# Moving attention's output product ahead of the values' block, and the loads of the input forms to GpSimd's queue

## The chip, the core and the metric

The kernel runs on one core of a Trainium2 chip. The core has TensorE (PE in the profile), VectorE (DVE), ScalarE (ACT), GpSimd (POOL) and SyncE (SP, which here only issues DMAs). Each engine works through its own instructions in a fixed order; they meet through semaphores. The metric is device time in microseconds (us), as the median of several runs. Before the change it is 1493.75 us, from three runs between 1492.93 and 1498.71.

## What is computed

A two-layer decoder over 512 tokens of width 1024, in float32. Each layer projects the normalized input, runs a sliding-window attention and a retention side by side, mixes both through gates, and ends in an MLP:

```python
h = rmsnorm(x, g_mix)
z = h @ w_in
aq, ak, av, rq, rk, rv, rg, ga, gb = jnp.split(z, SPLIT_POINTS, axis=-1)
ya = sliding_window_sink_attention(rope(aq), rope(ak), av, sinks) @ w_a
r = chunkwise_retention(rotate(rq), rotate(rk) * RET_QK_DIM ** -0.5, rv)
r = rms_per_head(r) * silu(rg)
mixed = sigmoid(ga) * ya + sigmoid(gb) * (r @ w_b)
x = x + mixed @ w_out
x = x + jnp.square(jax.nn.relu(rmsnorm(x, g_mlp) @ w_up)) @ w_down
```

A final RMSNorm follows the second layer. `w_in` has 5888 columns, `w_a` is 512 x 1024, and the values `rv` have 1024 columns.

## The kernel before

**Split products.** Every float32 matrix is split into a rounded part (hi) and the remainder (lo), and a product is the sum of three: hi by hi, lo by hi, hi by lo. These are lines 387, 388 and 389 of `products`. ACT rounds (line 335 for weights, 407 and 410 for activations), DVE subtracts (336, 408, 411).

**Weights.** They arrive in units of 128 x 1024 (512 KB) in a fixed order, given by `unit_order`. SP issues a load for each unit four units ahead (`load_until`, line 195, `load_values` line 309); the split runs three units ahead (`split_until`). There are five buffers for raw units and four each for hi and lo.

**Products by blocks.** The values' product and most of the MLP run as a 2 x 2 block product with seven partial products in place of eight. The operands of some of these are sums and differences of quarters of the input and of the weights. The input's quarters for the values' product are made by `Turned`: `load` brings two pairs of input chunks (tile `xg`, 512 KB each, from the input in layer 0 and from a copy in DRAM, `spill`, in layer 1), and `build` scales them on ACT (line 881), forms the combinations on DVE (884 to 887) and splits them (407, 408). There are two loads for `build(0)` and two for `build(2)`. The tiles `xg` share six buffers ("big") with other tiles of a layer: the attention's `whole`, the rg tiles `z`, the decay table `dm`. The weights' sums are made in DRAM by accumulating DMAs on GpSimd's queue (lines 223 and 226); `pace` issues one step of them after every second evacuation, behind a small copy (`mark`, line 247) that waits for that evacuation.

**The order within a layer.** First q, k and v of attention, then gate and retention chunks, between which a generator puts the steps of attention. After the generator is drained come `qk(1)` (retention keys and queries), the filling units rg 4 and 5, then `values` (the seven partial products, each over two units u and two banks m, tile `rv`), then attention's output product with `w_a` (8 products of 12 matmuls, evacuated into the gates on line 1131), and then `qk(2)` and `qk(3)` with the retention of heads 0 and 1 (`score`, `ret` and `r` rows) beside them. A list scheduler places the instructions on each engine by its own estimate of time, within the dependencies and within explicit `issue_after` marks. So the order on each engine isn't the order of the source, but it is fixed when the program is built.

**PSUM.** Eight banks: five in `ps_mm`, three in `ps_aux`. In a block product ACT copies the partial sum `a` into the bank `b` (line 954 for the values, 1405 in the MLP), and later matmuls add to it without opening a new group. A matmul that opens a group first (915 for the values; 1403 in the MLP, for the blocks listed in `CLEANED`) leaves that bank in a state in which they add. In the last layer, `turn_x` transposes x in front of the MLP into two banks, four transposes to a bank (line 1236).

Of the kernel before, what the change touches and what calls it, by code (L numbers as in the profile page):

```python
# [17 lines left out]
P = 128  # L18
# [32 lines left out]
DELAY = 2  # L51
AHEAD = 4
SPLIT = 3
CLEANED = ({1: (0,)}, {0: (0, 1), 1: (0,)})


def unit_order(layer):

    order = [("w_in", i) for i in range(4 + 2 + 8 + 2 + 4 + 2 + 2)]
    order += [("rv", part, u) for part in range(7) for u in range(2)]  # L60
    order += [("w_a", i) for i in range(4)]
    order += [("w_in", i) for i in range(24, 34)]
    order += [("w_b", i) for i in range(4)]
    order += [("w_in", i) for i in range(34, 38)]
    order += [("w_b", i) for i in range(4, 8)]
    order += [("w_out", i) for i in range(8)]
    for e in range(N_BLOCK):
        if e == 0:
            order += [("w_up", u) for u in range(4)]
        else:  # L70
            order += [("pair", 2 * e - 2 + i, part) for i in range(2) for part in range(4)]
        if layer == DEPTH - 1 and e == N_BLOCK - 1:
            order += [("w_end", k) for k in range(4)]
        else:
            order += [("block", e, part) for part in range(7)]
    return order
# [39 lines left out]
def decoder(ctx, tc, xT, x_first, w_in, w_rv, w_a, w_b, w_out, w_up, w_pair, w_down, w_end, tables, decay, band, g_last, out):  # L116
    nc = tc.nc
# [30 lines left out]
    x = little_x[:, P:].rearrange("p (k t) -> p k t", t=T)  # L148
# [13 lines left out]
    order = [(layer, *u) for layer in range(DEPTH) for u in unit_order(layer)]  # L162
# [209 lines left out]
    ident = const.tile([P, P], F32, name="ident")  # L372
# [31 lines left out]
    def split(hi, lo, src, scale=None):  # L404

        if scale is None:
            up = nc.scalar.activation(hi, src, AF.Copy)
            down = nc.vector.tensor_tensor(lo, src, f32(hi), ALU.subtract)
        else:
            up = nc.scalar.activation(hi, src, AF.Copy, scale=scale)  # L410
            down = nc.vector.scalar_tensor_tensor(lo, src, scale, f32(hi), ALU.mult, ALU.subtract)
        return up.ins, down.ins
# [198 lines left out]
    def layer_body(layer):  # L611
# [110 lines left out]
        a_h, a_l = a_t[0][0], a_t[1][0]  # L722

        def attention():
# [18 lines left out]
            def weighted(n):  # L743
                at = slice(n * P, (n + 1) * P)
                both = big("whole")
                rest, whole = both[:, 0, :], both[:, 1, :]
                for g in range(N_KV):
                    own, other = slice(64 * g, 64 * g + 64), slice(64 - 64 * g, 128 - 64 * g)
                    po = bank(ps_aux, "pv")
                    kbs = (1,) if n == 0 else (0, 1)  # L750
                    for kb in kbs:
                        b = n - 1 + kb
                        cols = slice(b * P, (b + 1) * P)
                        p = 2 * g + kb
                        nc.tensor.matmul(po, v_both[g][:, cols], p_h[:, p, :], start=kb == kbs[0], stop=False)
                        nc.tensor.matmul(po, v_high[g][:, cols], p_l[:, p, :], start=False, stop=kb == 1)
                    nc.scalar.activation(rest[own, :], po[other, :], AF.Copy)
                    nc.vector.tensor_tensor(whole[own, :], po[own, :], rest[own, :], ALU.add)
                split(a_h[:, :, at], a_l[:, :, at], whole.rearrange("p (c q) -> p c q", q=P))

            for n in range(NB):
                w = P if n == 0 else 2 * P
# [49 lines left out]
                slots.give(*t[1])  # L812
            slots.give(*k_s, *v_s)

        last_exp = []
        background.append(attention())


# [41 lines left out]
        class Turned:  # L860
# [6 lines left out]
            def load(self, ks):  # L867
                self.b = [big("xg") for _ in range(2)]
                for part, b in enumerate(self.b):
                    k = ks + 4 * part  # L870
                    nc.sync.dma_start(b, source[:, k : k + 2, :])

            def halves(self, ks, which):
                t = self.groups[which][ks // 2][0]
# [36 lines left out]
        def values(turned):  # L911

            a, c = ([bank(ps_mm, "rv") for _ in range(2)] for _ in range(2))
            b = [bank(pool, "rv") for pool in (ps_mm, ps_aux)]
            nc.tensor.matmul(b[1], ones, xh[:, 0, :], start=True, stop=True)
            plus, minus = rms_mix.columns, small.tile([P, NB], F32, tag="ncol", name="ncol", bufs=1)
            nc.vector.tensor_scalar(minus, plus, -1.0, None, ALU.mult)

            def multiply(ps, moving, start=True):
                for u in range(2):  # L920
                    hi, lo = unit("rv", layer)
                    for m in range(2):
                        at = slice(m * P, (m + 1) * P)
                        pairs = []
                        for k in range(2):
                            xh_, xl_ = moving[2 * u + k]
                            cols = slice(k * T, (k + 1) * T)
                            pairs.append(((xh_[:, at], xl_[:, at]), (hi[:, cols], lo[:, cols])))
                        products(ps[m], pairs, start and u == 0, u == 1, not start)

            def scale(j, m, sign):
                return (plus if sign > 0 else minus)[:, 2 * j + m : 2 * j + m + 1]

            def keep(j, ps, sign):
                got = []
                for m in range(2):
                    t = temp("kept")
                    nc.scalar.activation(t, ps[m], AF.Copy, scale=scale(j, m, sign))
                    got.append(t)
                return got  # L940

            def put(i, j, ps, sign, kept=None):
                for m in range(2):
                    hi, lo = slots.one(), slots.one()
                    if kept:
                        nc.vector.scalar_tensor_tensor(kept[m], ps[m], scale(j, m, sign), kept[m], ALU.mult, ALU.add)
                        split(view(hi), view(lo), kept[m])
                    else:
                        split(view(hi), view(lo), ps[m], scale(j, m, sign))
                    rv[i, 2 * j + m] = (hi, lo)  # L950

            multiply(a, quarter(0, 0))
            for m in range(2):
                nc.scalar.activation(b[m], a[m], AF.Copy)
            multiply(c, turned[1])
            five = keep(1, c, -1)
            multiply(b, turned[2], False)
            turned.free(0)
            two = keep(1, b, 1)
            multiply(a, quarter(1, 0), False)  # L960
            put(0, 0, a, 1)
            multiply(c, quarter(1, 1), False)
            put(0, 1, c, 1, two)
            multiply(b, turned[3], False)
            put(1, 1, b, -1, five)
            multiply(b, turned[4], False)
            turned.free(1)
            put(1, 0, b, -1)
# [95 lines left out]
        def load_decay(pair):  # L1064
            decays[pair] = big("dm")
            nc.sync.dma_start(decays[pair], decay[:, 2 * pair : 2 * pair + 2, :])

        def retention(pair):
            two = [Head(2 * pair), Head(2 * pair + 1)]
            for head in two:  # L1070
                for js in ((0, 1), (2, 3)):
                    head.scores(js)
                    yield
            two[0].outputs(0)
            yield
            two[0].outputs(1)
            yield
            two[1].outputs(0)
            yield
            yield  # L1080
            two[0].norm()
            yield
            two[1].outputs(1)
            yield
            yield
            yield
            two[1].norm()
            if pair == 0:
                load_decay(1)
            yield  # L1090
            yield
            while 4 * pair + 3 not in rg:
                yield
            for head in two:
                head.finish()
                yield
# [11 lines left out]
        turned = Turned()  # L1108
        turned.load(0)
        qk(1)  # L1110
        turned.build(0)
        turned.load(2)
        for i in (4, 5):
            chunk("w_in", layer, xs, put_rg(i))
        turned.build(2)
        load_decay(0)
        values(turned)


        aT = [(a_h[:, c, :], a_l[:, c, :]) for c in range(4)]  # L1120
# [12 lines left out]
        for t in a_t:  # L1133
            slots.give(*t[1])

        background.append(retention(0))
        qk(2, 2.0)
        qk(3, 2.0)
# [94 lines left out]

        def turn_x(ps, b, i):
            for k in range(4):
                nc.tensor.transpose(ps[:, k * P : (k + 1) * P], x[:, 4 * i + k, b * P : (b + 1) * P], ident)
            t = temp("y")
            nc.scalar.activation(t, ps, AF.Copy)
            nc.gpsimd.dma_start(y[:, b, i * T : (i + 1) * T], t)
# [542 lines left out]
```

## Time and profile before

| What | Before |
|---|---|
| median of three runs | 1493.75 us |
| the profiled execution, its own time | 1498.12 us |
| its span, first to last instruction | 1496.4 us |
| mean granted TensorE clock | 0.992 |
| DVE busy | 1125.0 us, 75% |
| ACT busy | 943.1 us, 63% |
| POOL busy | 217.4 us, 15% |

In the views quoted below, a row of the timeline gives its start, its duration, the engine, the line of the kernel, the operation, the tile written and the tile read, the shape and the count. A bracket holds the time that the engine sat idle before it and what ended that. In a row of stages, "from:to" is followed by the length of the stage, then busy time and count for PE, PE's weight loads, DVE, ACT and POOL, then the granted clock (1.00 is full), the share of the DMA engines that was busy, and GB/s. A row of waits gives the total in us, how often, and the longest. A row of the chain of work that ended last gives start, duration and what it was. A row for a DMA queue gives packets, MB and the share of 16 engines; a row for DMA issues gives the count, the size and the median time to landing. "q1 hardware_dynamic" carries what SP issues, "q0 software_dynamic" what POOL issues.

### The profile page before, as it was taken

How to read it: one execution, taken by the hardware profiler on the slowest of the kernel's cores; microseconds unless marked ns; L12 is line 12 of the kernel's file. 1: busy time of each engine (PE TensorE's matmuls, PEld its weight loads, DVE VectorE, ACT ScalarE, POOL GpSimd, SP SyncE). 2: the span in 40 equal slices, each digit the busy share in tenths (PEclk: the TensorE clock that was granted, in tenths of full speed). 3: DMA queues.
4: the chain of work that ended last, by engine and by line, in shares of the span. 5: the costliest groups of instructions: out<-in, count | busy, mean ns of one | idle time of the engine just before them, and what ended most of it. 6: DMA issues, size and time to landing. Idle time of an engine off the chain costs nothing.

```text
span 1496.4 us, 21384 instructions
## 1 busy us (share of the span) xinstructions
PE 1464.2 (98%) x7754; PEld 1260.4 (84%) x7754; DVE 1125.0 (75%) x1697; ACT 943.1 (63%) x1549; POOL 217.4 (15%) x294
## 2 busy tenths in 40 slices
PE   9999799999999999999999997999999999999998
PEld 7888588888888999999878885888888889999997
DVE  6878685875577888888778688668756768888885
ACT  7657554553467777777756576455434767777775
POOL 0101101202101111112201011112020021111120
PEclk9999899999999999999999999999999999999999
DMA  7673759568945776666947648677595287776664
GB/s 257 199 202 117 206 169 253 163 187 248 268 119 185 195 193 174 181 179 188 301 168 232 168 134 217 190 206 206 151 284 173 82 214 186 195 196 171 181 192 149
DMA packets 95867, 287.32 MB, mean 192 GB/s; under 512 B 11152, under 2 KB 11280, under 8 KB 90896
## 3 DMA queue, kind: packets, MB, share of 16 engines
q1 hardware_dynamic: 62544, 175.56, 33.6%
q0 software_dynamic: 32496, 109.07, 32.9%
q8 instruction: 61, 1.00, 0.3%
q10 hardware_dynamic: 720, 1.31, 0.2%
q14 instruction: 46, 0.38, 0.1%
HBM read 246.05 MB, written 107.48 MB: 236 GB/s over the span
## 4 chain that ended last, share of the span: by engine, by line
PE 92%; DMA 3%; ACT 2%; DVE 1%; issue 1%; ACTq 0%
PE mm L387 24%; PE mm L388 24%; PE mm L389 24%; PE b L387 3%; PE b L388 3%; PE b L389 3%; DMA xg<-xT_in 2%; PE rv L387 1%; PE rv L388 1%; PE rv L389 1%; PE mm L402 1%; PE score L770 1%; PE pT L735 1%; PE r L388 1%; DMA xg<-spill 1%; PE r L389 1%
## 5 line engine op out<-in xcount | busy, mean ns | idle before, releaser
L335 ACT ACTIVATE hi<-raw 128x1024 fp32r<-128x1024 f32 (+1 forms) x375 | 382.0, 1020 | 308.2 <-PE mm L388 178.4
L336 DVE TENSOR_TENSOR lo<-raw,hi 128x1024 fp32r<-128x1024 f32 (+1 forms) x376 | 438.8, 1174 | 151.4 <-ACT hi L335 150.0
L387 PE MATMUL mm<-xh,hi 128*128 128x512 f32 (+1 forms) x976 | 344.4, 355 | 1.8 <-DVE z L979 1.0
L388 PE MATMUL mm<-xl,hi 128*128 128x512 f32 (+1 forms) x976 | 343.7, 354 | 0.0
L389 PE MATMUL mm<-xh,lo 128*128 128x512 f32 (+1 forms) x976 | 341.9, 355 | 0.0
L388 PE MATMUL mm<-r,hi 128*128 128x256 f32 (+1 forms) x736 | 239.3, 325 | 0.0
L389 PE MATMUL mm<-r,lo 128*128 128x256 f32 (+1 forms) x736 | 238.4, 325 | 0.0
L387 PE MATMUL mm<-r,hi 128*128 128x256 f32 (+1 forms) x736 | 236.3, 325 | 0.5 <-ACT mm L1319 0.5
L387 PEld LDWEIGHTS mm<-xh,hi 128*128 128x128 f32 x976 | 184.8, 189 | 26.6 <-ACT xh L410 1.4
L388 PEld LDWEIGHTS mm<-xl,hi 128*128 128x128 f32 x976 | 184.9, 189 | 24.3
L389 PEld LDWEIGHTS mm<-xh,lo 128*128 128x128 f32 x976 | 183.9, 189 | 23.8
L387 PEld LDWEIGHTS mm<-r,hi 128*128 128x128 f32 x736 | 139.9, 190 | 14.0 <-ACT mm L1319 0.7
L388 PEld LDWEIGHTS mm<-r,hi 128*128 128x128 f32 x736 | 139.9, 190 | 13.0
L389 PEld LDWEIGHTS mm<-r,lo 128*128 128x128 f32 x736 | 139.9, 190 | 11.3
L1464 POOL DMA_DIRECT2D y<-eu x56 | 62.3, 1346 | 370.1 <-DVE eu L1449 370.1
L388 PE MATMUL mm<-lo,r 128*128 128x512 f32 (+1 forms) x276 | 104.4, 388 | 0.0
L389 PE MATMUL mm<-hi,r 128*128 128x512 f32 (+1 forms) x276 | 101.4, 387 | 0.0
L387 PE MATMUL mm<-hi,r 128*128 128x512 f32 (+1 forms) x276 | 98.7, 391 | 1.0 <-ACT eu L1459 0.6
L387 PE MATMUL b<-hi,r 128*128 128x512 f32 x180 | 70.6, 392 | 0.0
L388 PE MATMUL b<-lo,r 128*128 128x512 f32 x180 | 70.3, 391 | 0.0
L389 PE MATMUL b<-hi,r 128*128 128x512 f32 x180 | 67.9, 390 | 0.0
L271 DVE TENSOR_TENSOR raw<-raw 128x512 f32<-128x512 f32 x56 | 38.6, 690 | 37.0 <-DMA raw<-w_pair_in 27.9
(292 smaller groups left out, 2417.1 us busy)
## 6 DMA issues: line engine op xcount, KB each, us to landing
raw<-w_in_in SPq DMA_DIRECT2D x73, 512.0 KB, 5.5
sums_down<-w_down_in POOLq DMA_DIRECT2D x30, 1024.0 KB, 11.4
sums_up<-w_pair_in POOLq DMA_DIRECT2D x56, 512.0 KB, 9.7
raw<-w_down_in SPq DMA_DIRECT2D x45, 512.0 KB, 7.4
raw<-w_pair_in SPq DMA_DIRECT2D x84, 256.0 KB, 3.7
y<-y POOLq DMA_DIRECT2D x64, 256.0 KB, 9.3
y<-eu POOLq DMA_DIRECT2D x62, 256.0 KB, 8.3
raw<-sums_down SPq DMA_DIRECT2D x30, 512.0 KB, 7.2
```

The costliest lines, as they stand in the source:

```text
L271: nc.vector.tensor_tensor(raws[i][:, at], last[:, LEFT], last[:, RIGHT], ALU.add)
L335: nc.scalar.activation(hi[:, at], raw[:, at], AF.Copy)
L336: nc.vector.tensor_tensor(lo[:, at], raw[:, at], f32(hi[:, at]), ALU.subtract)
L387: nc.tensor.matmul(ps, ah, bh, start=start and i == 0, stop=False, **more)
L388: nc.tensor.matmul(ps, ah, bl, start=False, stop=False, **more)
L389: latest[0] = nc.tensor.matmul(ps, al, bh, start=False, stop=stop and i == n - 1, **more).ins
L402: latest[0] = nc.tensor.matmul(ps, w[:, cols(j, c)], moving[k][low], start=first, stop=bool(final)).ins
L735: nc.tensor.transpose(pt[:, i * P : (i + 1) * P], sm[:, at : at + P], ident)
L770: nc.tensor.matmul(ps[:, g * w : (g + 1) * w], q_s[g][:, c, at], part[:, keys], start=i == 0, stop=i == 1)
L1464: nc.gpsimd.dma_start(y[:, 2 * j + m, i * T : (i + 1) * T], t, **how)
```

## The change

Attention's output product now stands between the filling units and `values`; the order of the weight units follows. The loads of `xg` are issued by GpSimd in place of SP. Both builds are marked to be issued after the attention's last split (line 759). `load_decay(0)` moves with `values`. The transposes in `turn_x` become matmuls in transpose mode that form one group per bank: only the first opens it. The second layer's blocks are taken out of `CLEANED`, which removes three matmuls of line 1403 (each 128x512); the first layer keeps its one.

```diff
-CLEANED = ({1: (0,)}, {0: (0, 1), 1: (0,)})
+CLEANED = ({1: (0,)}, {})
...
     order = [("w_in", i) for i in range(4 + 2 + 8 + 2 + 4 + 2 + 2)]
+    order += [("w_a", i) for i in range(4)]
     order += [("rv", part, u) for part in range(7) for u in range(2)]
-    order += [("w_a", i) for i in range(4)]
...
-                split(a_h[:, :, at], a_l[:, :, at], whole.rearrange("p (c q) -> p c q", q=P))
+                last_split[:] = split(a_h[:, :, at], a_l[:, :, at], whole.rearrange("p (c q) -> p c q", q=P))
...
-                    nc.sync.dma_start(b, source[:, k : k + 2, :])
+                    nc.gpsimd.dma_start(b, source[:, k : k + 2, :])
...
         qk(1)
-        turned.build(0)
+        with tc.issue_after(last_split[0]), tc.issue_after(last_split[1]):
+            turned.build(0)
         turned.load(2)
         for i in (4, 5):
             chunk("w_in", layer, xs, put_rg(i))
-        turned.build(2)
-        load_decay(0)
-        values(turned)
+        with tc.issue_after(last_split[0]), tc.issue_after(last_split[1]):
+            turned.build(2)
...
         for t in a_t:
             slots.give(*t[1])
 
+        load_decay(0)
+        values(turned)
         background.append(retention(0))
...
             for k in range(4):
-                nc.tensor.transpose(ps[:, k * P : (k + 1) * P], x[:, 4 * i + k, b * P : (b + 1) * P], ident)
+                nc.tensor.matmul(
+                    ps[:, k * P : (k + 1) * P],
+                    x[:, 4 * i + k, b * P : (b + 1) * P],
+                    ident,
+                    start=k == 0,
+                    stop=k == 3,
+                    is_transpose=True,
+                    skip_group_check=True,
+                )
```

In the built program the loads stand on POOL as follows, in both layers: the first two behind an accumulating DMA of line 226, then a mark, a step of the sums, the third load, a mark, another step, and the fourth load. On SP the four units of `w_a` come where the first values' units were, and the decay table's load stands behind the fifth values' unit of the block, with five more behind it. On PE the two first score matmuls of the retention move ahead of the output product in layer 0.

More of the change, by code (lines that the diff above doesn't have):

```diff
@@ L813, in attention @@
             slots.give(*k_s, *v_s)
-        last_exp = []
+        last_exp, last_split = [], []
         background.append(attention())
```

## The prediction

> **What bounds the kernel now.** I read the page first (busy shares, chain), then who kept TensorE (PE) waiting, then PE's own rows around the values' block, and last the engines and queues that those waits name.
>
> ```profile
> span 1496.4 us, 21384 instructions
> PE 1464.2 (98%) x7754; PEld 1260.4 (84%) x7754; DVE 1125.0 (75%) x1697; ACT 943.1 (63%) x1549; POOL 217.4 (15%) x294
> PE 92%; DMA 3%; ACT 2%; DVE 1%; issue 1%; ACTq 0%
> ```
> PE is busy for 98% of the span and carries 92% of the chain that ends last. So an edit can win only what PE idles, what PE runs slowly, or matmuls that are removed. 32.2 us are idle (1496.4 - 1464.2). The waits of PE, and its rows that carry the longest, say where:
>
> ```profile
> PE rv L387 <- ACT hi L335: 6.3, 2, 4.8
> PE rv L387 <- ACT r L407: 5.9, 2, 4.5
> ...
> 171.41 1.27 PE L387 MATMUL rv<-hi,r 128*128 128x512 f32 x2 [5.69 <-ACT rv L954]
> 183.91 1.22 PE L387 MATMUL rv<-hi,xh 128*128 128x512 f32 x2 [4.78 <-ACT hi L335]
> 912.81 0.80 PE L387 MATMUL rv<-hi,r 128*128 128x512 f32 x1 [4.53 <-ACT r L407]
> 916.06 0.80 PE L389 MATMUL rv<-hi,r 128*128 128x512 f32 x1 [1.18 <-DVE r L408]
> 926.96 0.73 PE L387 MATMUL rv<-hi,xh 128*128 128x512 f32 x2 [1.49 <-ACT hi L335]
> 933.07 0.50 PE L387 MATMUL rv<-hi,r 128*128 128x512 f32 x1 [1.38 <-ACT r L407]
> ```
> Both waits, the longest two in the view, and all six rows belong to the values' block (tile rv); the rows add up to 19.05 us: 10.47 in layer 0, 8.58 in layer 1. They cost more than that, because PE comes back slow. Its normal pace is seen where the output product runs: the evacuation L1131 follows each product of 12 matmuls, 2.72 us after the one before, so 0.227 us a matmul.
>
> ```profile
> 232.03 0.69 DVE L1131 TENSOR_TENSOR x<-x,mm 128x512 f32<-128x512 f32 x1 [2.03 <-PE mm L389]
> ...
> 234.75 0.69 DVE L1131 TENSOR_TENSOR x<-x,mm 128x512 f32<-128x512 f32 x1 [0.63 <-PE mm L389]
> ```
> The three stretches behind the long waits, with PE's count and granted clock (seventh figure, 1.00 is full):
>
> ```profile
> 171.40:179.00 7.60, 7.54 (x24) 5.45 (x24) 3.61 (x5) 0.43 (x1) 1.54 (x3) 0.76 0.99 218
> 183.90:189.50 5.60, 5.59 (x15) 4.44 (x16) 5.60 (x9) 2.89 (x4) 0.00 (x0) 0.57 0.16 27
> 912.80:922.60 9.80, 8.47 (x25) 6.03 (x26) 9.19 (x13) 5.28 (x7) 2.55 (x5) 0.67 0.89 204
> ```
> Against 0.227 each they lose 7.60 - 24 x 0.227 = 2.15, 5.60 - 15 x 0.227 = 2.2, and 9.80 - 25 x 0.227 - 1.18 = 2.9: 7.3 us at a low clock. The block costs 26.3 us over its own work (19.05 + 7.3).
>
> Why does PE wait there? The names are ScalarE's (ACT), but ACT was itself held, in its own order, by loads of xg:
>
> ```profile
> 140.54 17.24 DMA xg<-xT_in
> ...
> 165.14 1.34 ACT L881 ACTIVATE xg<-xg,x 128x512 f32<-128x512 f32 x2 [3.11 <-DMA xg<-xT_in]
> ...
> 170.43 9.07 DMA xg<-xT_in
> ...
> 179.59 1.33 ACT L881 ACTIVATE xg<-xg,x 128x512 f32<-128x512 f32 x2 [7.76 <-DMA xg<-xT_in]
> ...
> 184.28 1.04 ACT L335 ACTIVATE hi<-raw 128x1024 fp32r<-128x1024 f32 x1
> 185.23 1.56 ACT L407 ACTIVATE r<-xg 128x512 fp32r<-128x512 f32 x2
> ...
> 924.62 1.33 ACT L881 ACTIVATE xg<-xg,x 128x512 f32<-128x512 f32 x2 [2.83 <-DMA xg<-spill]
> ```
> The second load takes 17.24 us; the third holds ACT until 165.14; the fourth cannot be issued before the first build gives its buffer back (170.43) and lands at 179.5. Everything behind it on ACT, weight roundings (L335) too, waits. The forms are rounded 7.3 us after that landing (179.5 to 186.8).
>
> **The output product moved ahead of the block.** Nothing is added on PE: per layer the same 96 matmuls stand earlier, 8 x 2.72 = 21.8 us, between the last filling unit (rg 5) and the use of the forms. They need the attention's last split, which lies before that point in both layers:
>
> ```profile
> 152.39 0.68 DVE L408 TENSOR_TENSOR r<-whole,r 128x512 fp32r<-128x512 f32 x1
> ...
> 158.68 0.39 PE L915 MATMUL rv<-xh,ones 128*128 128x512 f32 x1
> ...
> 897.96 0.69 DVE L408 TENSOR_TENSOR r<-whole,r 128x512 fp32r<-128x512 f32 x1
> ...
> 901.46 0.39 PE L387 MATMUL rv<-hi,xh 128*128 128x512 f32 x1
> ```
> The split ends at 153.1 and 898.7, PE arrives at 158.7 and 901.5: 5.6 and 2.8 us to spare, so this order costs nothing. If the split came later than that, PE would wait at the product's head. Putting the builds behind the split protects just this: on ACT and DVE the split no longer can stand behind a load.
>
> PE in layer 0 now: 158.7 + 21.8, plus 7 small items of the block and the first scores (7 x 0.227 = 1.6), plus the block's first 24 matmuls, 5.45, gives 187.5 for the first use of a form. Writing L for the landing of the fourth load, ACT has the three roundings of the forms done at L + 7.3, and in the changed program the weight that this product needs stands right behind them, 1.04: L + 8.3. The wait that is left is L + 8.3 - 187.5, so L - 179.2 where that is positive. In layer 1 PE arrives at 901.5 + 21.8 + 1.4 + 5.45 = 930.1, and what is left is L - 921.8. With L as before (179.5; 924.6) that is 0.3 + 2.8 = 3.1 us instead of 19.05, too short (nearest row: the 1.49 us wait) to bring the low clock.
>
> **The loads moved to GpSimd's queue.** SP loses a queue head that waits for buffers; the weights behind it come earlier, which PE does not feel while it is at the output product. But L changes: on POOL the loads stand behind the sums that are made in DRAM.
>
> ```profile
> 139.59 1.09 POOL L223 DMA_DIRECT2D sums_down<-w_down_in  x1
> 143.93 0.84 POOL L226 DMA_DIRECT2D sums_up<-w_pair_in  x1 [3.24 <-DMA sums_up<-w_pair_in]
> ...
> 152.15 0.82 POOL L226 DMA_DIRECT2D sums_down<-w_down_in  x1 [5.95 <-DMA sums_down<-w_down_in]
> ...
> q0 software_dynamic: 1440, 6.82, 55.2%
> q1 hardware_dynamic: 1008, 3.67, 20.3%
> ```
> The last two rows cover 138 to 190 us: POOL's queue q0 moves 6.82 MB in 55.2% of 52 us, 238 GB/s. The first two loads are issued after 143.93 (some 4.5 us later than now) behind at most 1.6 MB, 6.6 us: about when they land now. The third follows the 1 MB of 152.15: with its own 0.5 MB, 1.57 MB / 238 = 6.6 us, so 160 to 168, where 165.1 is now. The fourth is issued 5.3 us after the third lands (165.14 to 170.43) and takes 9.07 to 17.24: L lies between 174 and 190.5. I take 181, the third's landing a little later and the shorter, latest row. That leaves 1.8 in layer 0 and, with the same 1.5 us of delay, 4.3 in layer 1: 6 us. Bounds: 0, and 11.3 twice with the slow clock of 2.2 behind each, 27. What queues behind the waiting loads on POOL is the marks and further sums, needed only in the second half of a layer: no cost.
> The Trainium skill speaks against this step (DMA: Bandwidth & Descriptors, "Issuing engine by pattern" and "Specifications"): plain loads belong on Sync, whose path is generally faster, with about 0.6 us to the first byte against about 1 us from gpsimd; an estimate from that is 0.4 us more per load, under 1 us in the sum. No run here shows a plain load on both queues yet.
>
> **The cleaning matmuls and the transposes.**
>
> ```profile
> L1403 PE MATMUL b<-xh,ones x4: 389/392/502, 486.7 to 1232.8; 128*128 128x512 f32 x4
> ...
> ACT y L1238: 0.7, 2
> ...
> L1236 PE MATMUL xt<-ident,x x16: 272/273/273, 1181.4 to 1198.3; 128*128 128x128 f32 x16
> ```
> Three of the four go: 3 x 0.227 = 0.7, and the 0.7 of idle time before them; 0 to 1.4, I take 1. The 32 transposes keep their number and shape; a flag is no row here, so 0, with 0.1 either way on each (3 us) as the outer bound.
>
> **Work behind the block.** The retention follows it directly now, without the product's 21.8 us between. The three score and output stages have other chunks beside them and PE shows no wait there, so I allow 1 us; 0 to 5 is the bound, by what DVE had to do in the product's window beside L1131 (14.82 - 8 x 0.69 = 9.3, half of it weight splits that move along).
>
> ```profile
> 213.00:237.00 24.00, 24.00 (x107) 19.90 (x106) 14.82 (x20) 9.03 (x13) 5.36 (x8) 1.00 0.66 194
> ```
> **Sum.** 26.3 + 1 - 6 - 1 = 20.3 us. From the profiled execution: span 1496.4, own time 1498.1, so 1476 to 1478; that run lies 4.4 us over the median of 1493.75 and near the highest of the three, 1498.7. From the median it is 1473.4; I forecast 1474.
>
> **The rivals.**
> (a) The loads land late on the software queue: L near its upper bound once or in both layers. For it: 17.24 us for one load already, and 1 MB sums ahead in the same queue; against it: the bytes are the same, and 9.07 was the latest. Price 10 us more: 1484.
> (b) It doesn't do what it says: the wait follows the forms, all 11.3 + 2.2 per layer, 27 us. About 1494.
> (c) Slower: the decay table. Its load stands on SP among the values' weights and waits for a buffer of the forms. In the changed order, five weights of the block stand behind it.
>
> ```profile
> 189.42 0.33 SPq L1066 DMA_DIRECT2D dm<-decay_in  x1
> 191.69 0.33 SPq L309 DMA_DIRECT2D raw<-sums_rv  x1
> ...
> 189.50:213.00 23.50, 23.50 (x108) 19.60 (x107) 20.34 (x25) 14.20 (x18) 0.00 (x0) 1.00 0.66 218
> raw<-w_rv_in SPq DMA_DIRECT2D x2, 512.0 KB, 6.6
> ```
> Were they to land one after another at 6.6 us each, 33 us would stand against the 7 units that they serve (7 x 12 x 0.227 = 19): 14 us a layer, 28. With 6 left before and 4.4 of slow clock it gives back all 27.3 and 11 more: 1505. It decides once the table is issued more than some 10 us after PE reaches the forms. Against: the same queue head stood there before (189.42), the next weight was issued 2.3 us later, and PE was busy for 23.50 of 23.50 us.
>
> **How the numbers follow.** Forecast 0.66, (a) 0.18, (b) 0.08, (c) 0.08. Half a percent, 7.5 us, is what a measurement of this kernel tells from no change. Faster (below 1486.3): 0.66 and most of (a), 0.80; same: the rest of (a) and (b), 0.12; slower: (c), 0.08. The low end is 26.3 + 1.4 with nothing left, 1466; the high end takes in most of (a), 1488. The likeliest case alone: 1468 to 1481.
>
> **What would show it.** Right: no rv row of PE with more than 3 us of idle time before it, clock 1.00 through both blocks, PE idle near 15 us, mm of the output product ahead of rv, three fewer L1403. The landing of the fourth load (ACT's L881 row) checks L: 181 and 926. Wrong: L beyond 186, low clock behind the first form's product, idle PE rows at the head of the output product (split late) or at weights behind dm (c), or new waits in the retention.

## The result: 0.3% faster, and where the forecast gain went

| | before | after |
|---|---|---|
| median of 20 runs each | 1496.24 us | 1492.52 us |
| lowest to highest | 1491.39 to 1501.23 | 1489.49 to 1493.61 |
| the profiled execution, its own time | 1498.12 us | 1491.67 us |
| its span | 1496.4 us | 1489.9 us |

The ratio is 0.997, with a 95% interval of 0.9958 to 0.9982: a gain of some 4 us, where 20 were forecast. The profiled execution lies 1.9 us above the median before and 0.9 below it after, so the spans differ by more, 6.5 us. The stall of 26.3 us in the values' block went. Some 21 us of new waits and low clock came in two other places.

The first part of the page of the changed kernel, busy time and share:

```profile
PE 1461.6 (98%) x7751; PEld 1259.5 (85%) x7751; DVE 1121.9 (75%) x1697; ACT 942.6 (63%) x1549; POOL 215.5 (14%) x302
```

PE is still busy for 98%; idle are 28.3 us (1489.9 - 1461.6) in place of 32.2. The waits of PE show that these are other microseconds than before:

```profile
PE mm L387 <- DVE x L1131: 8.2, 2, 5.7
PE mm L387 <- ACT hi L335: 5.4, 2, 3.2
PE mm L389 <- DVE lo L336: 1.8, 3, 0.9
```

No row of rv is left in this view, while before the three longest were of rv. What waits now is mm. PE's own rows, with the idle time in the bracket, say where:

```profile
170.44 0.50 PE L387 MATMUL mm<-r,hi 128*128 128x512 f32 x1 [2.49 <-DVE x L1131]
...
220.58 0.50 PE L387 MATMUL mm<-xh,hi 128*128 128x512 f32 x1 [2.24 <-ACT hi L335]
222.19 0.50 PE L389 MATMUL mm<-xh,lo 128*128 128x512 f32 x1 [0.88 <-DVE lo L336]
...
909.17 0.79 PE L387 MATMUL mm<-r,hi 128*128 128x512 f32 x1 [5.73 <-DVE x L1131]
...
961.20 0.79 PE L387 MATMUL mm<-xh,hi 128*128 128x512 f32 x1 [3.17 <-ACT hi L335]
963.07 0.80 PE L389 MATMUL mm<-xh,lo 128*128 128x512 f32 x1 [0.64 <-DVE lo L336]
```

The rows at 170 and 909 lie inside the output product, which now runs ahead of the block. The other four lie at the end of the block, at `qk(2)`. The stretches behind them, with PE's count and, in the seventh figure, the granted clock:

```profile
170.44:175.00 4.56, 4.56 (x20) 3.82 (x21) 4.56 (x7) 2.19 (x4) 1.52 (x2) 1.00 1.01 284
909.17:915.00 5.83, 5.83 (x18) 4.68 (x19) 4.53 (x6) 3.17 (x5) 0.56 (x1) 0.70 0.99 263
961.20:968.00 6.80, 6.15 (x15) 4.47 (x16) 6.67 (x12) 2.78 (x5) 0.00 (x0) 0.55 0.57 180
220.58:223.00 2.42, 1.54 (x6) 0.97 (x7) 2.42 (x4) 1.48 (x3) 0.00 (x0) 1.00 0.76 254
223.00:230.00 7.00, 7.00 (x25) 5.62 (x24) 3.99 (x8) 1.30 (x3) 0.00 (x0) 0.76 0.49 151
```

Behind the wait of 2.49 us the clock stayed at 1.00: 20 matmuls in 4.56 us. At 0.227 us a matmul, as in the prediction, the low clock costs 5.83 - 18 x 0.227 = 1.7 behind the output product's wait in layer 1. Behind the waits at the block's end it costs 6.80 - 15 x 0.227 - 0.64 = 2.8 in layer 1 and 9.42 - 31 x 0.227 - 0.88 = 1.5 in layer 0. So the account is:

- the output product's wait: 2.49 + 5.73 + 1.7 = 9.9 us
- the wait at the block's end: 2.24 + 0.88 + 3.17 + 0.64 + 2.8 + 1.5 = 11.2 us
- together 21.1 of the 26.3 us; 5.2 remain, and the span fell by 6.5.

**The first wait.** The row at 909.17 names DVE's evacuation L1131. DVE's rows ahead of it:

```profile
902.48 0.69 DVE L884 TENSOR_TENSOR xg<-xg 128x512 f32<-128x512 f32 x1 [8.46 <-ACT xg L881]
...
907.24 0.68 DVE L887 SCALAR_TENSOR_TENSOR xg<-t,xg 128x512 f32<-128x512 f32 x1
...
908.44 0.68 DVE L1131 TENSOR_TENSOR x<-x,mm 128x512 f32<-128x512 f32 x1
```

In the order of the built program the output product's first evacuation stands behind the first build of the forms (884 to 887), and DVE idles 8.46 us at the head of that build until ACT has scaled a load of xg. In layer 0 the same wait of ACT, 6.71 us, holds DVE for 7.33 us just ahead of the build. The evacuation needs none of it, but it waits in line, and PE runs out of banks. So independent matmuls put ahead of the wait did not cover all of it: the matmuls are independent, their evacuations are not.

**The second wait.** The chain of work that ended last (start, duration, what) leads at both places to the values' weights, and the DMA view of 184 to 218 us shows what they shared the engines with:

```profile
203.40 13.97 DMA raw<-w_rv_in
217.48 1.07 ACT hi L335
...
929.51 11.77 DMA raw<-w_rv_in
...
945.01 10.79 DMA raw<-w_rv_in
```

```profile
q0 software_dynamic: 1123, 5.64, 67.3%
q1 hardware_dynamic: 1184, 4.35, 35.5%
...
raw<-w_rv_in SPq DMA_DIRECT2D x3, 512.0 KB, 10.1
raw<-sums_rv SPq DMA_DIRECT2D x2, 512.0 KB, 11.1
```

Before the change, 190 to 224 us cover the second half of the block and the start of the output product, with the same 155 matmuls. There q0 had no traffic at all, and weights landed in about 5 us:

```profile
q1 hardware_dynamic: 1728, 6.29, 55.5%
...
raw<-w_a_in SPq DMA_DIRECT2D x4, 512.0 KB, 4.3
raw<-w_rv_in SPq DMA_DIRECT2D x2, 512.0 KB, 5.7
```

The 5.64 MB are the weights' sums. `pace(mixed[c])` stands in the loop of the output product, eight times a layer, and every second call starts a step of the sums. Where the product went, four steps went with it. POOL's rows of both kernels show it, before first:

```profile
176.16 0.82 POOL L226 DMA_DIRECT2D sums_up<-w_pair_in  x1
222.90 1.04 POOL L247 COPY mark<-x 128x1 f32<-128x1 f32 x1 [45.92 <-DVE x L1131]
```

After:

```profile
176.10 0.79 POOL L247 COPY mark<-x 128x1 f32<-128x1 f32 x1
176.83 0.53 POOL L223 DMA_DIRECT2D sums_up<-w_pair_in  x1
...
202.65 0.81 POOL L226 DMA_DIRECT2D sums_down<-w_down_in  x1 [11.62 <-DMA sums_down<-w_down_in]
```

Before, POOL issued its last sums at 176.16, in the block's first half, and was then silent for 45.92 us, through the rest of the block. Now its marks wait for evacuations that come ahead of the block, and its copies run beside the block's weights. The Trainium skill (DMA: Bandwidth & Descriptors, "Queues, rings and completion order") says that each DMA engine takes turns between the queues that have work for it, a packet at a time. The rows agree as far as they go: q1's loads get through, in 10.1 and 11.1 us, about twice the 4.3 to 5.7 of before. The turns themselves no row shows.

### The profile page after: what moved, and what is told of

It is laid out like the page before. It is cut to its first block, busy times and chain, and to the rows that moved or that the text cites. A ratio compares the mean times of both kernels' runs of the same rounds, so it can differ in the third digit from the quotient of the medians.

```text
span 1489.9 us, 21378 instructions
## 1 busy us (share of the span) xinstructions
PE 1461.6 (98%) x7751; PEld 1259.5 (85%) x7751; DVE 1121.9 (75%) x1697; ACT 942.6 (63%) x1549; POOL 215.5 (14%) x302
## 3 DMA queue, kind: packets, MB, share of 16 engines
q0 software_dynamic: 33648, 113.26, 34.0%
## 4 chain that ended last, share of the span: by engine, by line
PE 86%; DMA 7%; ACT 3%; DVE 2%; issue 1%; POOL 0%; SPq 0%; ACTq 0%; DVEq 0%; POOLq 0%
PE mm L387 23%; PE mm L389 23%; PE mm L388 23%; PE b L387 3%; PE b L388 3%; PE b L389 3%; DMA raw<-w_rv_in 2%; DMA xg<-spill 1%; PE mm L402 1%; DMA xg<-xT_in 1%; PE score L770 1%; DVE lo L336 1%; DMA sums_down<-w_down_in 1%; ACT hi L335 1%; PE r L388 1%
```

## The experiments

The theory after the result: the moved `pace` calls make the second wait, the first build's place on DVE makes the first. The rivals: the loads' new queue, the order of issue on SP, the transposes and cleaning matmuls. All ratios are to the kernel before, on the chip of the same batch.

| Kernel | median us | ratio | 95% interval |
|---|---|---|---|
| after | 1492.52 | 0.997 | 0.9958 to 0.9982 |
| b_late_sums: after, sums behind the block | 1480.46 | 0.9896 | 0.9872 to 0.992 |
| j_late_again: the same, other chip | 1480.54 | 0.9902 | 0.9877 to 0.9927 |
| f_sums_in_block: before, sums beside the block | 1512.32 | 1.012 | 1.0099 to 1.0142 |
| a_sync: after, loads on SP | 1494.56 | 0.9997 | 0.9977 to 1.0017 |
| e_late_sums_sp: b, loads on SP | 1487.75 | 0.9954 | 0.9935 to 0.9974 |
| h_queue_alone: before, loads on GpSimd's queue | 1493.49 | 0.9992 | 0.998 to 1.0004 |
| c_builds_03: after, builds behind evacuations | 1498.01 | 1.002 | 1.0003 to 1.0036 |
| g_order_and_late: b, builds behind evacuations 2 and 5 | 1483.66 | 0.9927 | 0.991 to 0.9945 |
| i_order_early_late: b, builds behind evacuations 1 and 4 | 1487.6 | 0.9949 | 0.9934 to 0.9964 |
| d_turn_alone: before, transposes and cleaning only | 1493.97 | 0.9992 | 0.9973 to 1.0011 |

### The sums put back behind the block (b_late_sums, j_late_again)

The eight marks leave the output product's loop, and four more are made later, in the evacuations of `qk(2)` and `qk(3)`. Steps that are left over follow at the marks behind these; the page has 113.26 MB on q0, as in the changed kernel.

```diff
@@ the evacuation of retention's queries and keys
+                if h >= 2:
+                    pace(f32(view(hi)))
@@ the output product
-                pace(mixed[c])
```

> The changed kernel without the steps of the sums in DRAM that the output product's evacuations pace; as many marks fewer two steps are paced by the last four rotations of retention's keys and queries instead. Theory (the values' block now shares the DMA engines with four steps of sums, 5.6 MB on the software queue in 34 us, so its weights land in 10 to 12 us where they took 4 to 6): the waits for weights at the end of the block (5.4 on ACT hi, 1.5 on DVE lo, 4 at a low clock) go, raw<-w_rv lands in 4 to 7 us, time 1481 to 1485; the output product's wait of 8.2 stays. Rival (the weights are issued late, since DVE frees their buffers behind the builds): landing gets shorter but the waits stay above 4 us, time 1489 to 1493.

Measured: 1480.46 us. The DMA view of 184 to 218 us has no q0 any more, and each group of loads has a median of 3.7 us:

```profile
q1 hardware_dynamic: 1584, 5.77, 54.4%
...
raw<-w_rv_in SPq DMA_DIRECT2D x3, 512.0 KB, 3.7
raw<-sums_rv SPq DMA_DIRECT2D x2, 512.0 KB, 3.7
```

The longest wait of PE (L1133 is here what L1131 is in the changed kernel; the next is 1.3 us, at the MLP):

```profile
PE mm L387 <- DVE x L1133: 8.8, 2, 6.1
```

The second wait is gone and the first is as it was. Against the changed kernel this is (0.997 - 0.9896) x 1494 = 11 us, what the account gave that wait (11.2); the spans give 10.9 (1489.9 - 1479.0), while the two intervals by themselves leave 6 to 16. Same work, same bytes, other time: made later, the sums bring no new wait of note, and beside the block they cost some 11 us.

> The kernel of b_late_sums once more, on the chip of i_order_early_late: 1478 to 1483, its ratio to before inside 0.987 to 0.992 again.

It came out at 1480.54 us, 0.9902. In its profile the output product's wait is 6.7 us, where b_late_sums had 8.8: such a row can differ by some 2 us between two executions. This version beats both kernels.

### Only the sums beside the block (f_sums_in_block)

The kernel before, its output product in its old place; the eight marks are moved into the two builds, four each.

```diff
@@ Turned.build, at its end
+                for _ in range(4):
+                    pace(f32(self.groups[1][ks // 2][0][:, 0, :]))
@@ the output product
-                pace(mixed[c])
```

> The kernel before, with the output product where it was, and only the eight marks of its loop (four steps of the sums made in DRAM, per layer) moved into the two builds of the forms, so that the sums run beside the values' block. Theory (sums beside the block delay its weights): loads of weights in the block land 9 to 12 us after issue instead of 4 to 6, the software queue shows over 2 MB in the block's 34 us where it showed none, PE waits for a weight's rounding in the block's second half; 4 to 12 us slower, 1498 to 1507. Rival (the weights were late in the changed kernel for the order of issue on SP, not for the sums): landings stay at 4 to 6 us and the time within 2 us of 1494.6.

Measured: 1512.32 us, 15 to 21 us slower (0.0099 and 0.0142 x 1494); the forecast of 4 to 12 was too small, the direction right. The loads land late, as expected. The DMA view of 184 to 218 us:

```profile
q0 software_dynamic: 1188, 5.58, 69.3%
...
raw<-w_a_in SPq DMA_DIRECT2D x4, 512.0 KB, 18.2
...
dm<-decay_in SPq DMA_DIRECT2D x1, 512.0 KB, 18.9
```

Its longest wait, and the DVE row behind it:

```profile
PE ret L387 <- DVE s L1020: 11.5, 2, 6.1
```

```profile
213.48 1.16 DVE L1020 TENSOR_TENSOR s<-ret,dm 128x512 f32<-128x512 f32 x2 [5.18 <-DMA dm<-decay_in]
```

So the sums make the loads late without the new order of weights. But PE doesn't pay where it was expected to. Its waits in the values' block add up to 15.9 us, less than the 19.6 before; what is new is the wait for scores that need the decay table, 11.5 us in the two layers. In all PE is idle for 39.1 us (1510.8 - 1471.7) against 32.2, and the same 7754 matmuls keep it busy for 7.5 us longer (1471.7 - 1464.2): 14.4 us in the span, about half of it low clock. The run shows what the sums do to landings; its price is that of another load, and not to be set beside the 11 us.

### The loads' queue (a_sync, e_late_sums_sp, h_queue_alone)

One line, in the changed kernel (a_sync), in b_late_sums (e_late_sums_sp), and the other way in the kernel before (h_queue_alone):

```diff
-                    nc.gpsimd.dma_start(b, source[:, k : k + 2, :])
+                    nc.sync.dma_start(b, source[:, k : k + 2, :])
```

> The changed kernel with the loads of the input forms issued by SP again, as before. Theory (the queue is nearly indifferent; what matters is the order of evacuations on DVE and the sums in DRAM): first two loads issued some 4.5 us earlier, so the output product's wait for its evacuation (8.2 us in two rows) falls to 3 to 6; SP's head blocks again for buffers, so the weights at the block's end come no earlier and that wait stays at 5 to 8. Time 1488 to 1493. Rival (the software queue made the loads late, and that is what ate the gain): the output product's wait goes whole and the time falls to 1480 to 1484.

Measured: 1494.56 us, 0.9997. The output product's wait grew, where the expectation had it shrink, and the one at the block's end fell:

```profile
PE mm L387 <- DVE x L1131: 13.5, 2, 9.8
PE mm L389 <- DVE lo L336: 2.3, 3, 1.1
PE mm L387 <- ACT hi L335: 2.0, 2, 1.5
```

The two kernels' intervals overlap a little. So the queue was tried again without the sums in the block:

> The changed kernel with both edits: the sums kept behind the values' block (as in b_late_sums, 1480.5 us) and the loads of the forms on SP again (as in a_sync, 1494.6 us). Theory: with the sums gone from the block the queue of the loads is worth only what the first build's lateness makes of it; SP's loads made the output product wait 13.5 us against 8.2 us on GpSimd's queue, so 5 us more than b_late_sums: 1484 to 1488, and no wait at the end of the values' block. Rival (the queue matters by itself, plain loads are better on SP): 1474 to 1479. Rival (b_late_sums won only because its loads share GpSimd's queue with fewer sums): as a_sync, 1492 to 1496.

Measured: 1487.75 us, 0.9954 against 0.9896 and 0.9902 on GpSimd's queue, with intervals that don't meet: some 8 us worse, a little over the theory's 5. The wait is the same as in a_sync (13.4 us, longest 9.8), and no other is over 1.3 us. The run also tests the sums a second time, with the loads on SP in both kernels. Against a_sync the sums behind the block are worth (0.9997 - 0.9954) x 1494 = 6 us, and a_sync's 4.3 us of waits at the block's end are gone. So b_late_sums did not win only by clearing the loads' own queue.

DVE's first row of layer 1's build, in e_late_sums_sp and then in b_late_sums:

```profile
906.48 0.69 DVE L886 TENSOR_TENSOR xg<-xg 128x512 f32<-128x512 f32 x1 [12.51 <-ACT xg L883]
```

```profile
897.50 0.69 DVE L886 TENSOR_TENSOR xg<-xg 128x512 f32<-128x512 f32 x1 [8.78 <-ACT xg L883]
```

The forms' data come 3.7 us later from SP (12.51 - 8.78): in the chain of work that ended last, the load that ACT waits for takes 20.63 us from SP and 16.95 from POOL. A difference that the traces show: SP issues the third load of layer 1 at 891.06, 7.4 us after the first two (883.64), while on POOL it stands behind an accumulating copy, at 888.90, 10.6 us after them (878.29). That this is why the first two land later isn't shown; no run separates it.

> The kernel before with the loads of the forms on GpSimd's queue and nothing else. Theory: the values' block still waits for its forms; the first two loads are issued at much the same time, the third and fourth are not held behind weights on SP, so the stall of 19.05 us shrinks by 0 to 6 us: 1489 to 1495. Rival (plain loads are slower on this queue, and stand behind the sums): the forms land 5 us later, 1498 to 1506.

Measured: 1493.49 us, 0.9992 with 1.0 in the interval: the queue alone is worth nothing that can be told here. The rv waits are still there (10.9 and 4.7 us in the two largest groups). The Trainium skill (DMA: Bandwidth & Descriptors, "Issuing engine by pattern"), by which plain loads belong on Sync, isn't borne out here: without the other edits no difference, with them 8 us the other way.

### The builds behind the evacuations (c_builds_03, g_order_and_late, i_order_early_late)

If the evacuations stand behind the build, put the build behind an evacuation. In c_builds_03 (and, with the sums kept out of the block, in i_order_early_late) the builds come after tiles 0 and 3 of the output product; in g_order_and_late after tiles 1 and 4.

```diff
-        with tc.issue_after(last_split[0]), tc.issue_after(last_split[1]):
-            turned.build(0)
-        turned.load(2)
@@ the output product, tile c
-                nc.vector.tensor_tensor(mixed[c], mixed[c], ps, ALU.mult)
+                done = nc.vector.tensor_tensor(mixed[c], mixed[c], ps, ALU.mult)
+                if c in (0, 3):
+                    with tc.issue_after(last_split[0]), tc.issue_after(done.ins):
+                        turned.build(0 if c == 0 else 2)
+                    if c == 0:
+                        turned.load(2)
```

> The changed kernel with build(0) marked behind the evacuation of the output product's first product and build(2) behind that of the fourth; third and fourth load follow the first build. Theory (the output product waits because its evacuations and those of rg 4 and 5 stand behind build(0) on DVE, and build(0) behind a load that lands at 161 and 901 us): the row of 8.2 us falls below 2, its low clock goes; but the third load is issued later, so a wait of 0 to 6 us a layer comes back at the first use of the second build's forms. The wait for weights at the end stays. Time 1482 to 1490. Rival (banks are short for another reason): the row of 8.2 us stays above 6, time 1490 to 1494.

Measured: 1498.01 us. The waits of PE:

```profile
PE rv L387 <- ACT rv L954: 13.8, 1, 13.8
PE rv L387 <- DVE x L1126: 9.4, 1, 9.4
```

This is outside both expectations. The output product's wait went, so its cause was the place of the builds; but the block waits again, 23.2 us. In layer 1, 13.8 us are the old stall: ACT copies rv only behind its waits for xg. In layer 0, 9.4 us are new: one of the product's last evacuations (L1126) now stands inside the second build. The wait for weights at the block's end, which was expected to stay, is not in the view. The third load is written behind the first build, and so stands on POOL behind more marks and sums; POOL's rows of layer 1:

```profile
911.61 0.46 POOL L247 COPY mark<-r 128x1 f32<-128x1 f32 x1 [11.94 <-ACT r L407]
...
920.37 0.60 POOL L871 DMA_DIRECT2D xg<-spill  x1
...
925.65 1.78 POOL L871 DMA_DIRECT2D xg<-spill  x1
```

In the changed kernel the fourth had landed by 917.

> The changed kernel with the sums kept behind the values' block, and the first build behind the evacuation of the output product's second tile, the second build behind that of its fifth. Theory: the output product no longer waits for its evacuations (8.8 us in b_late_sums gone), but the third and fourth loads are issued later, so PE waits at the first use of a form instead; 1478 to 1490, about 1484, with rv waits of 3 to 8 us a layer. Rival (the marks between the loads on GpSimd's queue, not the builds' place, hold the loads): rv waits of over 9 us a layer as in c_builds_03, 1488 to 1496.

> As g_order_and_late, with the first build behind the evacuation of the output product's first tile and the second behind that of its fourth, so that the last two loads are issued one tile (2.7 us) sooner. Theory (the waits behind the product follow the landing of the last loads): the rv waits of 6.5 us fall to 0 to 3 and the output product waits under 2 us; 1477 to 1483, level with or a little under the kernel with the sums alone put back. Rival (the product's last evacuations stand behind the second build on VectorE, whatever its loads): the rv waits stay at 6 us or grow, 1483 to 1488.

Measured: 1483.66 and 1487.6 us. In both the output product no longer waits, and rv does, for the product's last evacuations behind the second build: 6.5 us in g_order_and_late, 8.5 in i_order_early_late, which also waits 2.7 us for a form's rounding. The edit of i_order_early_late did not bring what it was meant to: the last two loads are issued at 911.48 and 913.13 us in layer 1, in g_order_and_late at 911.21 and 913.52. With the loads no sooner, only the second build stands further ahead of the product's evacuations, and that made the wait longer, as the rival had it. None of the three beats b_late_sums: the wait for the loads of xg moves, and doesn't go.

### The transposes and the cleaning matmuls alone (d_turn_alone)

> The kernel before with the transposes as one group per bank and without the three cleaning matmuls alone. Theory: three matmuls of 0.227 us and at most 0.7 us of idle time before them: 0 to 1.4 us faster, ratio 0.999 to 1.000. Rival (the cleaning matmuls fill time in which PE would wait anyway, for ACT's evacuation in the first block of the last layer): 0 to 0.5 us, and the wait of 0.56 us there grows by about what was removed.

Measured: 1493.97 us, 0.9992, which a gain of 1 us and none both fit. Its waits of PE have this row, which the changed kernel has too:

```profile
PE mm L387 <- ACT eu L1467: 1.3, 1, 1.3
```

Its place is 1194 us, behind the removed matmuls. Before, the wait for eu was 0.56 us. PE arrives sooner, by three matmuls of 0.227 us, and waits 0.7 us longer for the same activation.

## Why the prediction fell short, step by step

**The stall and what it would give: right.** No rv row of PE waits in the changed kernel, and the 26.3 us are gone in all versions that keep the builds ahead of the product's evacuations (after, a_sync, b_late_sums, e_late_sums_sp, j_late_again). PE idle near 15 us, the other sign that was named, did not come: it is 28.3. A total of 3.1 us of waits was taken as too short to bring the low clock; in the new places 2.24 and 0.88 us were followed by a clock of 0.76, and 3.17 and 0.64 by 0.55.

**The landing of the loads: better than forecast.** The fourth load was taken to land at 181 and 926. The chain and ACT's row show it earlier:

```profile
911.46 5.21 DMA xg<-spill
```

```profile
176.77 1.34 ACT L881 ACTIVATE xg<-xg,x 128x512 f32<-128x512 f32 x2 [2.18 <-DMA xg<-xT_in]
```

That is 176.8 and 916.7. The third came within its bounds in layer 0 (167.6 of 160 to 168), the fourth took 5.2 us in layer 1 where 9.07 was taken. So the 6 us set aside for a wait that is left were not spent, and rival (a) fell.

**"This order costs nothing": the first step that failed.** The sentence checked what the output product reads, the attention's split, and not what takes its results away: the wait for an evacuation was put at nothing. Its evacuations share DVE with the build, and the builder's order put the build first. Cost: 9.9 us; c_builds_03, g_order_and_late and i_order_early_late, which change that place, have no such wait. The rows were there: the prediction's own row has the second load, one of the two that the first build needs, landing at 157.8 (140.54 + 17.24), and took it to land about then again. In that kernel DVE then finishes the build's forms at 165.9 (L887), while the output product's first result would be due at 161.4, 2.72 us after PE gets there.

**"What queues behind the waiting loads on POOL is the marks and further sums ... no cost": the second.** The sums aren't needed early, that is true. But the question was which transfers they would run beside. The output product carries eight marks, and four steps of the sums move with it; the DMA view of the old block had no q0 traffic to warn of it: with q0 silent the weights landed in 4 to 6 us, and in 3.7 in b_late_sums. Cost: 11.2 us by the trace, 11 by b_late_sums.

**Cleaning and transposes, 1 us: not seen.** The wait for eu took it.

**Work behind the block, 1 us: no row of PE's waits shows it.** What does wait there, `qk(2)`, waits for weights.

**The rivals.** (b) comes nearest in time, 1494, but not by its mechanism: the wait didn't follow the forms. (c) had the place right, weights at the end of the block, and the cause wrong: not the queue head of the decay table but the sums. Where the sums were alone (f_sums_in_block) the decay table did come late, by 5.18 us at DVE's row, because it took 18.9 us to land.

With the second failure undone, the forecast becomes 1474 - 6 (not spent) + 9.9 = 1478; b_late_sums has 1480.5. The two terms of 1 us, for the transposes and for the work behind the block, were both not seen and cancel.

**Open.** Why loads issued by SP land later in the changed order. And how the last 7 to 9 us of the output product's wait could go: an evacuation on an engine that no load holds up was not tried.

## What to carry to other kernels

- When a block of independent matmuls is moved to cover a wait, follow its results as well as its operands: the engine that empties its banks must not be the one that stands in the wait.
- Look for everything that is paced by the moved loop. A call that starts a background transfer is a transfer that moves, and its price depends on whose loads it lands beside.
- A queue that is silent in a tight stretch may be why that stretch works.

## What was not expected of the hardware

Copies and accumulating copies from DRAM to DRAM on GpSimd's queue delay SP's loads: with 5.64 MB of them in 34 us a 512 KB load took 10 to 12 us in place of 3.7, and with 5.58 MB in f_sums_in_block 11.5 to 18.9. The total went up at the same time, windows of 184 to 218 us in the changed kernel and then in b_late_sums (the last two figures are the DMA engines' share and GB/s):

```profile
184.00:218.00 34.00, 34.00 (x155) 28.31 (x153) 24.64 (x26) 16.37 (x20) 4.08 (x7) 1.00 1.03 295
```

```profile
184.00:218.00 34.00, 34.00 (x154) 28.30 (x153) 28.63 (x30) 19.18 (x24) 0.00 (x0) 1.00 0.55 170
```

That a load finds free engines at a share of 0.55 and has to queue at 1.03 is a reading of these rows, not shown: no run separates the share from the kind of copies. PE is busy all 34 us in both: the block lives off the weights split ahead, and the delay shows only at its end, at 220 us.
